# First six input blocks multiplied with x ahead of its norm: a fused two-block kernel on Trainium2

## Chip, cores and metric

One Trainium2 chip, one core. The metric is device microseconds (us) of one execution; lower is better. The engines are named as in the profile: PE (TensorE matmul), PEld (its weight loads), DVE (VectorE), ACT (ScalarE), POOL (GpSimd), SP (SyncE, which issues nearly all transfers).

## What is computed

Two transformer blocks on 512 tokens of width 1024, in float32. The part that the change touches is the start of the first block (the reference, cut):

```python
def rms_norm(x, g):
    y = xf * lax.rsqrt(jnp.mean(xf * xf, axis=-1, keepdims=True) + RMS_EPS)
    return (y * g).astype(x.dtype)

h = rms_norm(x, norm_mix)
p = h @ w_in                                   # 5,408 columns
p_rw = p_rw + (token_shift(p_rw) - p_rw) * mu_shift
r, k, v, wd, ad, gd, cb, cc, cx, ga, gb = jnp.split(p, offsets, axis=-1)
out_a = rwkv7_branch(r, k, v, wd, ad, gd, ...)   # a recurrence over tokens
out_b = short_conv_branch(cb, cc, cx, conv_w)
merged = sigmoid(ga + bg_a) * (out_a @ w_proj_a) + sigmoid(gb + bg_b) * (out_b @ w_proj_b)
x = x + merged @ w_out_mix
```

After this come cross-attention to a memory of 256 tokens, an MLP, and the second block (windowed attention and spatial gating). The norm's factor belongs to a token, so that (x * norm_mix) @ w_in can be multiplied by it afterwards, column by column of the transposed product.

## The kernel before

**Layout.** Activations lie transposed: 128 features on the partitions, 512 tokens along a row, eight such tiles for 1024 features. w_in is held as 43 blocks of 128 output columns. Each block is one `proj_in(blk)` (L228): eight contraction steps j of three matmuls 128x512 into one PSUM bank, 24 in all. The three are the terms of a float32 product in split form (`mm_fm`, L179): high part times high part (L182), weight-high times activation-low (L183), weight-low times activation-high (L184). `wload` (L168) fetches a block's weights in two halves of 256 KB (DMA L174 on SP's queue, five buffers `wraw`), and `split` (L150) makes of each half a high part by an ACT cast (L152, `whi`, four buffers) and a low part by a DVE subtraction (L153, `wlo`, three). With `early` POOL makes that subtraction (tiles `we`).

**Banks.** Three PSUM banks (`mm`) take these products, two (`sc`) sums, broadcasts and transposes, three (`ch`) the recurrence. A product may begin when the bank that it takes has been read out.

**Order.** A scheduler fixes each engine's instruction stream at build time, and an engine runs its stream strictly in that order. A wait at one instruction therefore holds all that stands behind it on that engine.

**The start.** x arrives in four transfers of 512 KB (`x0`, L120), then the first weights. ACT squares the eight x tiles (L203, L206), DVE and POOL add them into two accumulators (L207, L208), `sums` (L142) lets PE sum over the partitions, `rsqrt` (L130) takes eleven small DVE steps, `bcast` (L189) spreads the result over the partitions through PE, and eight DVE steps `hx` (L212) scale x, each split into `h`. Only then can a block of w_in begin, since every product reads `h`.

**The blocks.** Block 0 holds the two low-rank inputs, 1 and 2 the gate's; `prep(j)` (L283) for j = 0 to 3 takes three blocks for k, r and v, each followed by `shift` (L233: an ACT scaling `q`, then one DVE step L237 that mixes a token with the one before). `prep` also has head sums (L292), a low-rank product (`lora_mm`, L274), a broadcast (L314) and a chain of DVE and POOL steps that ends in `rkk` (L332). `prep_tail(j)` (L337) sums rkk (L340) and transposes v (`vs`, L344) on PE. After the fourth, 24 matmuls make the output gate gt (L369 to L371).

**The recurrence** runs in eight chunks of 64 tokens: `gram` (L386), an inverse that DVE iterates, and `chunk` (L431, matmuls L443 to L491), where each step waits for a DVE or ACT result. To keep PE busy the scheduler sets matmuls of independent blocks between those steps: gate b (blocks 15 to 22, tiles `bt`, L553), the convolution (23 to 34), w_proj_b and gate a (35 to 42, `tga`). After it come transposes of the memory (L586) and the product w_k.

Of the kernel before, what the change touches and what calls it, by code (L numbers as in the profile page):

```python
# [19 lines left out]
D = 1024  # L20
# [25 lines left out]
def fused_kernel(ctx, tc, a, out):  # L46
# [19 lines left out]
    def regionr(name):  # L66
        return reg.tile([128, 4, 2, T], F32R, tag="R", bufs=7, name=nm(name))
# [4 lines left out]
    def tt(name, shape=(128, T), dt=F32):  # L72
        return tp.tile(list(shape), dt, tag="t", bufs=10, name=nm(name))
# [4 lines left out]
    def mmbank():  # L78
        return ps.tile([128, T], F32, tag="mm", bufs=3, name=nm("mm"))
# [4 lines left out]
    def chbank():  # L84
        return ps.tile([128, T], F32, tag="ch", bufs=3, name=nm("ch"))
# [30 lines left out]

    vc = cst.tile([128, NVEC], F32, name="vc")
    x0 = reg.tile([128, DB, T], F32, tag="R", bufs=7, name="x0")
    for i in range(4):
        nc.sync.dma_start(x0[:, 2 * i:2 * i + 2], a["xT"][:, 2 * i:2 * i + 2])  # L120
        if i == 0:
            nc.sync.dma_start(vc, a["vecs"])

    def vcol(name, i=0, n=1):
        o = VOFF[name] + i
        return vc[:, o:o + n]
# [31 lines left out]
    def wsplit(raw, shape, early=False):  # L158
        if early:
            w = reg.tile([128, 2] + shape[1:], F32R, tag="G4", bufs=4, name=nm("we"))  # L160
            split(raw, w[:, 0], w[:, 1], eng=G)
            return w[:, 0], w[:, 1]
# [5 lines left out]
    def wload(tiles, k0, nk, early=False):  # L168
        ncol = tiles.shape[2]
        step = T // ncol  # L170
        parts = []
        for k in range(k0, k0 + nk, step):
            raw = wp.tile([128, step, ncol], F32, tag="wraw", bufs=5, name=nm("wraw"))
            nc.sync.dma_start(raw, tiles[:, k:k + step, :])  # L174
            hi, lo = wsplit(raw, [128, step, ncol], early)
            parts += [(hi[:, i, :], lo[:, i, :]) for i in range(step)]
        return parts

# [18 lines left out]
    hreg = [regionr("h0"), regionr("h1")]  # L197
    h = pairs(hreg, DB)
    accx = [tt("accx"), tt("accx")]
    for j in range(DB):  # L200
        acc = accx[j % 2]
        if j < 2:
            S.activation(acc, x0[:, j], AF.Square)  # L203
        else:
            sq = tt("sqx")
            S.activation(sq, x0[:, j], AF.Square)  # L206
            (V, G)[j % 2].tensor_tensor(acc, acc, sq, op=ALU.add)  # L207
    V.tensor_tensor(accx[0], accx[0], accx[1], op=ALU.add)  # L208
# [980 lines left out]
```

## Time and profile before

| | us |
|---|---|
| three runs | 1343.22, 1336.71, 1340.09 |
| median | 1340.09 |
| the profiled execution | 1343.95 |
| its span in the trace | 1342.1 |

The granted clock of PE over the span is 0.989 of full speed. PE is busy for 97% of the span, DVE for 61%, ACT for 39%, POOL for 13%. The chain of work that ended last is PE for 94%. How to read it: the page gives shares over the whole span, the waits say which engine stood still for what, the windows give busy time and granted clock of a stretch, and the timeline lists instructions by their start, where several of one form that follow each other are one row with their count.

### The profile page before, as it was taken

To read this page: it belongs to the slowest core of one execution; us is meant where nothing else is said; L and a number is where in the kernel's file an instruction comes from. 1 tells how busy PE (TensorE), PEld (TensorE's weight loads), DVE (VectorE), ACT (ScalarE), POOL (GpSimd) and SP (SyncE) were. 2 spreads that over 40 slices of the span, in tenths; PEclk is the share of its full clock that TensorE was granted. 3 is DMA by queue.
4 is the path that set the end of the run, shared out by engine and by line. 5 is a ranking of instruction groups with operands and counts; after the bars stand their busy time and mean duration, and the time that the engine had idled before them with its cause. 6 is when DMAs were issued, how large, how long until landed. Compare 5 with 4: busy or idle time off the path is not lost.

```text
span 1342.1 us, 18317 instructions
## 1 busy us (share of the span) xinstructions
PE 1302.3 (97%) x6626; PEld 1069.7 (80%) x6626; DVE 814.8 (61%) x1631; ACT 520.5 (39%) x940; POOL 174.4 (13%) x184
## 2 busy tenths in 40 slices
PE   3999999999999999999999999999999999999997
PEld 2777888888879888888888888888878777788886
DVE  5677484848466755566854645535676656663455
ACT  4444232322335443454532423323344465333342
POOL 5113002010120010002012020020232000100003
PEclk9999999989999999999999999999999999999999
DMA  4222331314314532143643634332234223233331
GB/s 143 87 79 67 101 104 43 110 44 123 90 63 150 173 110 94 64 149 94 186 152 110 194 112 145 128 96 87 94 126 142 79 63 125 87 97 101 94 118 63
DMA packets 85210, 143.95 MB, mean 107 GB/s; under 512 B 21472, under 2 KB 21600, under 8 KB 85120
## 3 DMA queue, kind: packets, MB, share of 16 engines
q1 hardware_dynamic: 85120, 142.78, 34.0%
q8 instruction: 52, 0.85, 0.3%
q14 instruction: 38, 0.31, 0.1%
HBM read 136.19 MB, written 5.24 MB: 105 GB/s over the span
## 4 chain that ended last, share of the span: by engine, by line
PE 94%; DVE 3%; POOL 1%; DMA 1%; issue 0%; ACT 0%; SPq 0%; DVEq 0%; ACTq 0%; POOLq 0%
PE mm L182 26%; PE mm L183 26%; PE mm L184 25%; PE mm L627 1%; PE mm L628 1%; PE mm L629 1%; PE sc L386 1%; PE ch L943 1%; PE ch L978 1%; PE ch L458 1%; PE ch L467 1%; DMA x<-in_xT 1%; PE sc L974 1%; PE ch L462 1%; PE ch L491 1%; PE ch L474 1%
## 5 line engine op out<-in xcount | busy, mean ns | idle before, releaser
L152 ACT CAST whi<-wraw 128x512 fp32r<-128x512 f32 x406 | 251.7, 621 | 551.7 <-PE mm L183 475.7
L153 DVE TENSOR_TENSOR wlo<-wraw,whi 128x512 fp32r<-128x512 f32 x406 | 298.4, 736 | 228.1 <-PE mm L184 118.6
L182 PE MATMUL mm<-h,whi 128*128 128x512 f32 x328 | 132.5, 404 | 1.0 <-DVE k L237 1.0
L183 PE MATMUL mm<-h,whi 128*128 128x512 f32 x328 | 131.4, 401 | 0.0
L184 PE MATMUL mm<-h,wlo 128*128 128x512 f32 x328 | 131.1, 400 | 0.0
L182 PE MATMUL mm<-x2g,whi 128*128 128x512 f32 x256 | 100.2, 391 | 0.0
L184 PE MATMUL mm<-x2g,wlo 128*128 128x512 f32 x256 | 99.7, 389 | 0.0
L183 PE MATMUL mm<-x2g,whi 128*128 128x512 f32 x256 | 99.6, 389 | 0.0
L182 PE MATMUL mm<-ff,whi 128*128 128x512 f32 x256 | 99.6, 389 | 0.0
L183 PE MATMUL mm<-ff,whi 128*128 128x512 f32 x256 | 99.6, 389 | 0.0
L184 PE MATMUL mm<-ff,wlo 128*128 128x512 f32 x256 | 99.6, 389 | 0.0
L182 PEld LDWEIGHTS mm<-h,whi 128*128 128x128 f32 x328 | 62.8, 192 | 16.2 <-DVE k L237 2.6
L183 PEld LDWEIGHTS mm<-h,whi 128*128 128x128 f32 x328 | 62.7, 191 | 13.1 <-issue 0.4
L184 PEld LDWEIGHTS mm<-h,wlo 128*128 128x128 f32 x328 | 62.5, 190 | 13.3 <-issue 0.5
L852 POOL TENSOR_TENSOR X<-X,d 128x512 f32<-128x512 f32 x24 | 39.3, 1637 | 220.8 <-DVE d L850 220.8
L658 POOL TENSOR_TENSOR gt<-gt,nsq 128x512 f32<-128x512 f32 x21 | 27.7, 1320 | 291.5 <-ACT nsq L657 284.0
L183 PE MATMUL mm<-h2a,whi 128*128 128x512 f32 x152 | 59.7, 393 | 0.4 <-DVE h2a L875 0.4
L184 PE MATMUL mm<-h2a,wlo 128*128 128x512 f32 x152 | 59.8, 393 | 0.0
L182 PE MATMUL mm<-h2a,whi 128*128 128x512 f32 x152 | 59.7, 395 | 0.0
L182 PE MATMUL mm<-h2b,whi 128*128 128x512 f32 x152 | 59.7, 392 | 0.0
L184 PE MATMUL mm<-h2b,wlo 128*128 128x512 f32 x152 | 59.5, 393 | 0.0
L183 PE MATMUL mm<-h2b,whi 128*128 128x512 f32 x152 | 59.5, 392 | 0.0
(465 smaller groups left out, 2700.7 us busy)
## 6 DMA issues: line engine op xcount, KB each, us to landing
wraw<-in_w_in SPq DMA_DIRECT2D x162, 256.0 KB, 2.6
wraw<-in_w_up SPq DMA_DIRECT2D x64, 256.0 KB, 2.6
wraw<-in_w_down SPq DMA_DIRECT2D x64, 256.0 KB, 2.8
adaraw<-in_w_ada SPq DMA_DIRECT2D x24, 512.0 KB, 3.7
wraw<-in_w_proj_b SPq DMA_DIRECT2D x16, 256.0 KB, 2.7
wraw<-in_w_k SPq DMA_DIRECT2D x16, 256.0 KB, 2.6
wraw<-in_w_proj_a SPq DMA_DIRECT2D x16, 256.0 KB, 2.7
wraw<-in_w_v SPq DMA_DIRECT2D x16, 256.0 KB, 2.7
```

The lines of the kernel that those rows point to most:

```text
L152: S.copy(hi, src)
L153: eng.tensor_tensor(lo, src, hi.bitcast(F32), op=ALU.subtract)
L182: PE.matmul(acc, lhsT=wh, rhs=xh, start=start and k == 0, stop=False)
L183: PE.matmul(acc, lhsT=wh, rhs=xl, start=False, stop=False)
L184: PE.matmul(acc, lhsT=wl, rhs=xh, start=False, stop=stop and k == n - 1)
L386: PE.matmul(pq[hd % 2][:, j * 128:(j + 1) * 128], lhsT=KB[p0:p0 + 64, j, n * 128:(n + 1) * 128], rhs=AR[p0:p0 + 64, j, n].rearrange("p q c ...
L458: PE.matmul(pu[ub:ub + 32, hs], lhsT=ZT[ub:ub + 32, c, hd, :], rhs=gsb[ub:ub + 32, hs], start=True, stop=True)
L462: PE.matmul(pg[ub + 32:ub + 64, hd * 64:(hd + 1) * 64], lhsT=gr[ub:ub + 32, hd, 32:64], rhs=VU[ub:ub + 32, tb, c, hd, :], start=False, sto ...
L467: PE.matmul(pu[ub + 32:ub + 64, hs], lhsT=ZT[ub + 32:ub + 64, c, hd, :], rhs=gsb[ub + 32:ub + 64, hs], start=True, stop=True)
L474: PE.matmul(pst[:, j * 128:(j + 1) * 128], lhsT=KBt[:, 2 * j:2 * j + 2, :].rearrange("p h f -> p (h f)"), rhs=VU[:, tb, c, 2 * j:2 * j + 2 ...
L658: G.tensor_tensor(self.acc, self.acc, sq, op=ALU.add)
L852: G.tensor_tensor(X[:, j], X[:, j], d, op=ALU.add)
```

## The change

Line numbers from here on are those of the changed file where a row of the order of instructions says so; elsewhere they are those of the kernel before.

- x arrives in six transfers (four of one tile, 256 KB, and two of 512 KB), with the first halves of the weights of blocks 0 to 5 between them and the second halves behind (`first_weights`, buffers `wraw`).
- `split` takes x itself with norm_mix as the scale (ACT makes the high part of x * norm_mix, DVE the low part: tiles `xg`), and the six blocks accumulate (`first_mm`) into six banks, the three `mm` and the three `ch`, one contraction step of all six after the other as x lands. The 12 weight halves are split into areas of their own (`wf`, and `we`).
- The squares are added up by DVE alone, one accumulator. Their `sums` stands on PE behind the fourth contraction step, the broadcast behind the fifth.
- The broadcast is copied to SBUF (`rxs`, ACT), DVE makes hx and h of all eight tiles, and after them six DVE multiplications (`pf`) that scale the six finished products out of their banks. `shift` of blocks 0 to 5 reads `pf` in SBUF in place of a bank.
- Gate b's blocks 15 and 16 stand ahead of block 0's shift, block 17 ahead of the fourth `prep_tail`, the other five where all eight stood.
- The `early` path with POOL's subtractions is gone.

No product is left out: PE's stream has 5466 rows in both (a row may be several matmuls of one form).

```diff
+NFIRST = 6
...
-    for i in range(4):
-        nc.sync.dma_start(x0[:, 2 * i:2 * i + 2], a["xT"][:, 2 * i:2 * i + 2])
+    nc.sync.dma_start(x0[:, 0], a["xT"][:, 0])
+    nc.sync.dma_start(vc, a["vecs"])
+    first_weights(0, 0)
+    first_weights(1, 0)
+    nc.sync.dma_start(x0[:, 1], a["xT"][:, 1])
+    for i, j in ((2, 2), (3, 3), (4, 4), (5, 6)):
+        first_weights(i, 0)
+        nc.sync.dma_start(x0[:, j:min(j + 2, DB) if j > 3 else j + 1],
+                          a["xT"][:, j:min(j + 2, DB) if j > 3 else j + 1])
+    for i in range(NFIRST):
+        first_weights(i, 1)
...
-    accx = [tt("accx"), tt("accx")]
+    first = [mmbank() for _ in range(3)] + [chbank() for _ in range(3)]
+    accx = tt("accx")
+    def first_split(half):
+        w4 = regionr("wf")
+        for blk in range(NFIRST):
+            if blk < 4:
+                w = w4[:, blk]
+            else:
+                w = reg.tile([128, 2, T], F32R, tag="G4", bufs=4, name=nm("we"))
+            split(raw0[blk, half].rearrange("p k c -> p (k c)"), w[:, 0], w[:, 1])
+            wf_[blk, half] = w
+    def first_mm(j):
+        for blk in range(NFIRST):
+            w = wf_[blk, j // 4]
+            cs_ = slice((j % 4) * 128, (j % 4 + 1) * 128)
+            mm_fm(first[blk], [(w[:, 0, cs_], w[:, 1, cs_])], [xg[j]], start=j == 0, stop=j == DB - 1)
     for j in range(DB):
-        acc = accx[j % 2]
...
+        split(x0[:, j], xg[j][0], xg[j][1], scale=vcol("norm_mix", j))
+        if j % 4 == 0:
+            first_split(j // 4)
...
-            (V, G)[j % 2].tensor_tensor(acc, acc, sq, op=ALU.add)
-    V.tensor_tensor(accx[0], accx[0], accx[1], op=ALU.add)
-    rxb = bcast(rsqrt(sums(accx[0]), TB, 1.0 / D, 1e-6))
+            V.tensor_tensor(accx, accx, sq, op=ALU.add)
+        if j < DB // 2:
+            first_mm(j)
+    ssx = sums(accx)
+    first_mm(DB // 2)
+    rxb = bcast(rsqrt(ssx, TB, 1.0 / D, 1e-6))
+    for j in range(DB // 2 + 1, DB):
+        first_mm(j)
+    rxs = tt("rxs")
+    S.copy(rxs, rxb)
     for j in range(DB):
         hf = tt("hx")
-        V.scalar_tensor_tensor(hf, x0[:, j], vcol("norm_mix", j), rxb, op0=ALU.mult, op1=ALU.mult)
+        V.scalar_tensor_tensor(hf, x0[:, j], vcol("norm_mix", j), rxs, op0=ALU.mult, op1=ALU.mult)
         split(hf, h[j][0], h[j][1])
+    pf = []
+    for blk in range(NFIRST):
+        f = tt("pf")
+        V.tensor_tensor(f, first[blk], rxs, op=ALU.mult)
+        pf.append(f)
...
+    def proj_in(blk):
+        if blk < NFIRST:
+            return pf[blk]
...
+    gate_b(0)
+    gate_b(1)
     sa = tt("sa")
-    shift(proj_in(0, True), 12, sa)
+    shift(proj_in(0), 12, sa)
...
         tail = prep(j, tail)
+    gate_b(2)
     prep_tail(3, *tail)
...
-    for j in range(DB):
-        S.activation(bt[:, j], proj_in(15 + j), AF.Tanh, bias=hbg[:, 8 + j:9 + j], scale=0.5)
+    for j in range(3, DB):
+        gate_b(j)
```

How the order of PE's instructions stands at three places. In its rows `mm_`, `sc_` and `ch_` are banks, and the numbers only tell one use of a name from another.

PE at the end of the first `prep`, kernel before (mm_541 is block 5, v of j = 0; L340 and L344 are prep_tail(0); L274 is the second low-rank product; mm_656 is r of j = 1):

```order
L184 MATMUL mm_541<-h_3_113,wlo_551 128x512
L340 MATMUL sc_582<-hsel,rkk_496 128x2 x4
L344 MATMUL sc_588<-ident,vs_498 128x128 x4
L274 MATMUL mm_618<-wa,lhl 128x512
L274 MATMUL mm_619<-wa,lhl 128x512
L182 MATMUL mm_656<-h_2_112,whi_659 128x512
```

The same place in the changed file (mm_638 is block 6, k of j = 1; L332 is the second low-rank product; L398 and L402 are prep_tail(0); mm_753 is r of j = 1):

```order
L195 MATMUL mm_638<-h_43_386,wlo_648 128x512
L332 MATMUL mm_715<-wa,lhl 128x512
L332 MATMUL mm_716<-wa,lhl 128x512
L398 MATMUL sc_679<-hsel,rkk_630 128x2 x4
L402 MATMUL sc_685<-ident,vs_632 128x128 x4
L193 MATMUL mm_753<-h_42_385,whi_756 128x512
```

Before, block 4 and block 5 (r and v of j = 0) stand between the chain's start and L340; now they are done long ahead, and of whole blocks only block 6 stands between the first low-rank product and L398.

PE at the end of the fourth `prep`, before (mm_1105 is v of j = 3, L369 to L371 the gate gt):

```order
L184 MATMUL mm_1105<-h_3_113,wlo_1115 128x512
L369 MATMUL mm_1172<-whi_1161,gsp_255 128x512
L340 MATMUL sc_1146<-hsel,rkk_1102 128x2 x4
L370 MATMUL mm_1172<-whi_1161,gsp_255 128x512
L371 MATMUL mm_1172<-wlo_1162,gsp_255 128x512
```

And in the changed file (mm_1243 is gate b's block 17, 24 matmuls of which the last two stand here; L428 to L430 are the gate gt):

```order
L194 MATMUL mm_1243<-h_43_386,whi_1252 128x512
L195 MATMUL mm_1243<-h_43_386,wlo_1253 128x512
L398 MATMUL sc_1281<-hsel,rkk_1199 128x2 x4
L402 MATMUL sc_1287<-ident,vs_1201 128x128 x4
L428 MATMUL mm_1307<-whi_1296,gsp_535 128x512
```

A whole block now stands between v of j = 3 and the sum over its rkk, where one matmul stood.

PE in the last chunk of the recurrence, before (L447 to L491 are the chunk's steps, mm_3655 is one of the last blocks of gate a):

```order
L458 MATMUL ch_2405<-gsb_2404,ZT_2129 32x64 x8
L182 MATMUL mm_3655<-h_2_112,whi_3658 128x512
L183 MATMUL mm_3655<-h_2_112,whi_3658 128x512
L184 MATMUL mm_3655<-h_2_112,wlo_3659 128x512
L182 MATMUL mm_3655<-h_2_112,whi_3658 128x512
L183 MATMUL mm_3655<-h_2_112,whi_3658 128x512
L462 MATMUL ch_2391<-VU,gram_2002 32x64 x8
```

And in the changed file (L517, L521, L526 and L550 are the chunk's steps L458, L462, L467 and L491; mm_3779 is the last block of gate a, L644 transposes of the memory, mm_3819 the first block of w_k):

```order
L517 MATMUL ch_2540<-gsb_2539,ZT_2264 32x64 x8
L644 MATMUL sc_3720<-ident,mt_2584 128x128 x4
L194 MATMUL mm_3779<-h_43_386,whi_3788 128x512
L644 MATMUL sc_3765<-ident,mt_2588 128x128 x4
L521 MATMUL ch_2526<-VU,gram_2137 32x64 x8
L195 MATMUL mm_3779<-h_43_386,wlo_3789 128x512
L526 MATMUL ch_2540<-gsb_2539,ZT_2264 32x64 x8
L193 MATMUL mm_3819<-memhl,whi_3822 128x256
L550 MATMUL ch_2506<-VU,gram_2137 64x64 x8
```

Of the independent blocks 83 matmuls still stood behind L491 of the last chunk, 16 amid its steps; now gate a's last block ends amid them, and w_k begins.

## Rows read from the trace of the kernel before

**Rows 1.** Page, busy time (share of the span) and instructions by engine.
```profile
PE 1302.3 (97%) x6626; PEld 1069.7 (80%) x6626; DVE 814.8 (61%) x1631; ACT 520.5 (39%) x940; POOL 174.4 (13%) x184
```
**Rows 2.** Waits of PE: instruction <- releaser: us in total, times, longest.
```profile
PE sc L146 <- DVE accx L208: 17.0, 1, 17.0
PE sc L192 <- DVE rq_y L139: 4.1, 2, 3.4
PE sc L340 <- DVE rkk L332: 2.3, 1, 2.3
...
PE ch L447 <- DVE state L481: 1.3, 1, 1.3
...
PE mm L182 <- DVE k L237: 1.0, 1, 1.0
```
**Rows 3.** Windows: busy time and count by engine, granted clock, transfer share, GB/s.
```profile
core 0: us, PE busy (x) PEld busy (x) DVE busy (x) ACT busy (x) POOL busy (x), PEclk, DMA share, GB/s
...
10.00:15.00 5.00, 0.00 (x0) 0.00 (x0) 2.88 (x3) 3.42 (x6) 4.90 (x5) 1.00 0.91 263
...
0.00:25.78 25.78, 3.91 (x16) 3.56 (x16) 10.33 (x26) 10.14 (x17) 13.44 (x32) 1.00 0.60 186
25.78:30.00 4.22, 4.22 (x10) 3.19 (x11) 4.22 (x7) 3.10 (x6) 1.79 (x3) 1.00 0.00 0
30.00:40.00 10.00, 10.00 (x45) 8.26 (x44) 7.10 (x13) 3.56 (x7) 2.06 (x3) 1.00 0.34 109
...
53.00:57.00 4.00, 4.00 (x15) 3.22 (x15) 1.84 (x11) 0.33 (x1) 0.00 (x0) 0.59 0.00 0
...
132.00:139.00 7.00, 6.89 (x23) 5.85 (x24) 1.62 (x3) 1.22 (x3) 1.91 (x4) 0.52 0.17 59
```
**Rows 4.** Timeline of the start: start, duration, instruction, count, idle before it.
```profile
4.88 1.15 ACT L203 ACTIVATE accx<-x 128x512 f32<-128x512 f32 x2 [2.80 <-DMA x<-in_xT]
9.38 0.69 DVE L207 TENSOR_TENSOR accx<-accx,sqx 128x512 f32<-128x512 f32 x1 [3.52 <-ACT sqx L206]
15.11 5.40 POOL L153 TENSOR_TENSOR we<-wraw,we 128x512 fp32r<-128x512 f32 x4
15.19 1.74 DVE L208 TENSOR_TENSOR accx<-accx,accx 128x512 f32<-128x512 f32 x1 [1.16 <-POOL accx L207]
24.33 2.06 DVE L212 SCALAR_TENSOR_TENSOR hx<-x,vc,sc 128x512 f32<-128x512 f32 x3 [2.23 <-PE sc L192]
26.31 1.89 DVE L153 TENSOR_TENSOR h<-hx,h 128x512 fp32r<-128x512 f32 x3
```
**Rows 5.** Timeline of the first `prep`, PE and DVE.
```profile
52.68 0.95 PE L292 MATMUL sc<-hsel,sq 128*128 128x2 f32 x8
57.10 0.69 DVE L153 TENSOR_TENSOR wlo<-wraw,whi 128x512 fp32r<-128x512 f32 x1 [1.25 <-PE mm L184]
66.56 0.74 DVE L237 SCALAR_TENSOR_TENSOR r<-mm,omu,q 128x512 f32<-128x512 f32 x1
67.82 1.69 DVE L332 SCALAR_TENSOR_TENSOR rkk<-r,vc,f 128x512 f32<-128x512 f32 x1
72.93 0.96 PE L274 MATMUL mm<-wa,lhl 64*128 64x512 f32 x6
```
**Rows 6.** Timeline of the end of the fourth `prep`.
```profile
129.37 0.39 PE L369 MATMUL mm<-whi,gsp 128*128 128x512 f32 x1
130.30 1.66 DVE L332 SCALAR_TENSOR_TENSOR rkk<-r,vc,f 128x512 f32<-128x512 f32 x1
132.10 1.74 PE L340 MATMUL sc<-hsel,rkk 128*128 128x2 f32 x8 [2.35 <-DVE rkk L332]
142.08 1.16 PE L386 MATMUL sc<-AR,KB 64*128 64x128 f32 x16
```
**Rows 7.** Timeline of PE in the last chunk.
```profile
382.33 0.76 PE L447 MATMUL ch<-state,AR 128*64 128x128 f32 x5 [1.26 <-DVE state L481]
391.36 1.15 PE L491 MATMUL ch<-VU,gram 128*64 128x64 f32 x16
```

More of the change, by code (lines that the diff above doesn't have):

```diff
@@ L118, in fused_kernel, with first_weights @@
     x0 = reg.tile([128, DB, T], F32, tag="R", bufs=7, name="x0")
-    for i in range(4):
-        nc.sync.dma_start(x0[:, 2 * i:2 * i + 2], a["xT"][:, 2 * i:2 * i + 2])
-        if i == 0:
-            nc.sync.dma_start(vc, a["vecs"])
+    raw0 = {}
+    def first_weights(blk, half):
+        w = wp.tile([128, 4, 128], F32, tag="wraw", bufs=5, name=nm("wraw"))
+        nc.sync.dma_start(w, a["w_in"][blk][:, 4 * half:4 * half + 4, :])
+        raw0[blk, half] = w
+    nc.sync.dma_start(x0[:, 0], a["xT"][:, 0])
[9 more added lines that the diff above has]
+        first_weights(i, 1)
     def vcol(name, i=0, n=1):
@@ L156, in split, with wsplit @@
             V.scalar_tensor_tensor(lo, src, scale, hi.bitcast(F32), op0=ALU.mult, op1=ALU.subtract)
[L158 to L162, printed above, removed]
+    def wsplit(raw, shape):
         hi = wp.tile(shape, F32R, tag="whi", bufs=4, name=nm("whi"))
@@ L166, in wsplit, with wload @@
         return hi, lo
-    def wload(tiles, k0, nk, early=False):
+    def wload(tiles, k0, nk):
         ncol = tiles.shape[2]
@@ L174, in wload @@
             nc.sync.dma_start(raw, tiles[:, k:k + step, :])
-            hi, lo = wsplit(raw, [128, step, ncol], early)
+            hi, lo = wsplit(raw, [128, step, ncol])
             parts += [(hi[:, i, :], lo[:, i, :]) for i in range(step)]
@@ L194, in bcast @@
         return p
-    hreg = [regionr("h0"), regionr("h1")]
-    h = pairs(hreg, DB)
-    accx = [tt("accx"), tt("accx")]
-    for j in range(DB):
-        acc = accx[j % 2]
-        if j < 2:
-            S.activation(acc, x0[:, j], AF.Square)
+    xgr = [regionr("xg0"), regionr("xg1")]
+    xg = pairs(xgr, DB)
+    first = [mmbank() for _ in range(3)] + [chbank() for _ in range(3)]
+    accx = tt("accx")
+    wf_ = {}
+    def first_split(half):
[12 more added lines that the diff above has]
+            mm_fm(first[blk], [(w[:, 0, cs_], w[:, 1, cs_])], [xg[j]], start=j == 0, stop=j == DB - 1)
+    for j in range(DB):
+        split(x0[:, j], xg[j][0], xg[j][1], scale=vcol("norm_mix", j))
+        if j % 4 == 0:
+            first_split(j // 4)
+        if j == 0:
+            S.activation(accx, x0[:, j], AF.Square)
         else:
@@ L206, in fused_kernel @@
             S.activation(sq, x0[:, j], AF.Square)
-            (V, G)[j % 2].tensor_tensor(acc, acc, sq, op=ALU.add)
-    V.tensor_tensor(accx[0], accx[0], accx[1], op=ALU.add)
-    rxb = bcast(rsqrt(sums(accx[0]), TB, 1.0 / D, 1e-6))
+            V.tensor_tensor(accx, accx, sq, op=ALU.add)
[8 more added lines that the diff above has]
+    S.copy(rxs, rxb)
+    hreg = [regionr("h0"), regionr("h1")]
+    h = pairs(hreg, DB)
     for j in range(DB):
         hf = tt("hx")
-        V.scalar_tensor_tensor(hf, x0[:, j], vcol("norm_mix", j), rxb, op0=ALU.mult, op1=ALU.mult)
+        V.scalar_tensor_tensor(hf, x0[:, j], vcol("norm_mix", j), rxs, op0=ALU.mult, op1=ALU.mult)
         split(hf, h[j][0], h[j][1])
+    pf = []
[3 more added lines that the diff above has]
+        pf.append(f)
     omu = cst.tile([128, 15], F32, name="omu")
@@ L226, in fused_kernel @@
     V.tensor_scalar(hbg, vcol("b_gate", 0, 16), 0.5, None, op0=ALU.mult)
-    def proj_in(blk, early=False):
+    def proj_in(blk):
+        if blk < NFIRST:
+            return pf[blk]
         p = mmbank()
-        mm_fm(p, wload(a["w_in"][blk], 0, DB, early), h)
+        mm_fm(p, wload(a["w_in"][blk], 0, DB), h)
         return p
@@ L237, in shift, with gate_b @@
         V.scalar_tensor_tensor(dst, p, omu[:, mi:mi + 1], q[:, 0:T], op0=ALU.mult, op1=ALU.add)
+    bt = reg.tile([128, DB, T], F32, tag="R", bufs=7, name="bt")
+    def gate_b(j):
+        S.activation(bt[:, j], proj_in(15 + j), AF.Tanh, bias=hbg[:, 8 + j:9 + j], scale=0.5)
+    gate_b(0)
+    gate_b(1)
     sa = tt("sa")
-    shift(proj_in(0, True), 12, sa)
+    shift(proj_in(0), 12, sa)
     S.activation(sa[0:64], sa[0:64], AF.Tanh)
@@ L254, in fused_kernel @@
         sg = tt("sg")
-        shift(proj_in(1 + i, i == 0), 13 + i, sg)
+        shift(proj_in(1 + i), 13 + i, sg)
         S.activation(sg, sg, AF.Tanh, scale=0.5)
@@ L551, in fused_kernel @@
         post(tb)
-    bt = reg.tile([128, DB, T], F32, tag="R", bufs=7, name="bt")
-    for j in range(DB):
-        S.activation(bt[:, j], proj_in(15 + j), AF.Tanh, bias=hbg[:, 8 + j:9 + j], scale=0.5)
+    for j in range(3, DB):
+        gate_b(j)
     ob = regionr("ob")
```

## The prediction

> **What bounds the kernel now.** I read the page's busy times first: PE works 97% of the span, DVE 61% [rows 1]. So the time is PE's work plus what PE loses by standing still or by its slower clock, and a change that keeps the number of matmuls, as this one does, can only win or lose in those two. The waits of PE come next [rows 2]. One wait towers: 17.0 us at the start for the sum of squares, then 3.4 us for the rsqrt chain. In the windows PE is busy 3.91 us of the first 25.78 [rows 3], so 21.9 us are lost before the first block. Two smaller waits lie further on, 1.0 us for k and 2.3 us for rkk at the end of the fourth `prep`, and 1.3 us in the recurrence.
>
> The clock shows in the pitch of the matmuls: 10 in 4.22 us just after the start, 0.42 us each, against 45 (and 44 weight loads) in 10.00 us later [rows 3], 0.222 to 0.227, which I take as 0.2255. These are the 1.2 and the 2.4 GHz level. After the 2.3 us wait the granted clock is 0.52 for the 7 us from 132 to 139 [rows 3]. An idle stretch therefore costs its own length and a slow stretch behind it.
>
> **The start.** x in tiles of 256 KB lets work begin early, but 3.5 MB (x and six half blocks) must land before the last of the first four steps' inputs is there. At 263 GB/s [rows 3] that takes 13 us after a first landing near 4 (4.88 with 512 KB pieces [rows 4]), so about 16.7. Meanwhile ACT has 29 casts and squares at 0.57 (two squares in 1.15 [rows 4]), 16.5 us, done near 23. DVE has 20 splits of x and weights and 7 additions, 27 at 0.63 (three in 1.89, one alone 0.69 [rows 4]), 17 us; with waits for data it has the last sum near 25. POOL leaves this stage, and with it the slow DVE steps beside POOL (1.74 in place of 0.69 [rows 4]).
>
> PE first gets scattered matmuls from about 6 us, is fed without gaps from 13.5 and, as before, spends some 4 to 5 us at the 0.42 pitch. I take the fourth step's end at 28. Then: column sums 0.95, fifth step 18 x 0.2255 = 4.1, broadcast 1.0, three steps 54 x 0.2255 = 12.2. The six blocks are done at 46.1. The rsqrt chain (3.4 us [rows 2]) lies beside the fifth step's 4.1, which covers it by 0.7. DVE makes h and `pf` (8 scalings, 8 subtractions, 6 multiplications, 22 x 0.66 = 14.5) from 34.6 to 49, beside the last three steps; the first bank is free near 45.5, when gate b's block 15 wants it. If that cover were gone it would cost 1 to 2 us.
>
> Gate b's two blocks follow, 48 x 0.2255 = 10.8, to 57.0. Then both low-rank products, head sums and broadcast (0.96 [rows 5], 0.96, 0.95, 1.05), block 6 (5.4), and a short wait for the bank that gate b's tanh empties (0.3): 66.6 at the end of the second low-rank product. Before, PE was there at 72.93 + 0.96 = 73.9 [rows 5], without gate b's 10.8 of work but with 1.5 of `prep_tail(0)` (head sums and transposes) that now lies behind. So PE is **ahead by 73.9 + 10.8 - 1.5 - 66.6 = 16.6 us**. The 21.9 us that were idle don't all come back, since data, casts and the slow clock still hold PE until about 18.
>
> **A new wait behind it.** L398 now needs rkk, and what ran beside that chain before, blocks 4 and 5 (10.8 us), is done already. From head sums to the end of rkk it took 69.51 - 52.68 = 16.8 us [rows 5], of which DVE stood 1.25 for PE. With the sums at 57.0, rkk is ready near 72.6. PE arrives at 66.6: **6.0 us idle**. Queued behind L398 are the v transposes and block 7; three `mm` banks are held by block 6 and the second low-rank product, so nothing else could run. I charge **2.8 us** for the slower clock behind it, a little under the 3.3 lost by 7 us at 0.52 [rows 3]. From here the order is that of before, period by period.
>
> One rule speaks against this step. r and v are now shifted out of SBUF instead of a bank, so that DVE reads two SBUF operands there. A step that reads two SBUF operands beside POOL is the last addition of squares, 1.74 us in place of 0.69 [rows 4], while `shift` from a bank takes 0.74 [rows 5]. I leave r at 0.74, since POOL's step of the same chain may be over by then; the other end is 1.0 more idle.
>
> The Trainium skill, page "SBUF — State Buffer", section "SBUF: two separate sides", says that a DVE step with two SBUF inputs and a GpSimd step that reads SBUF exclude each other for their whole length; the row of 1.74 agrees, and by it alone the sum below would be 1 us smaller.
>
> **The fourth `prep_tail`.** From 129.37 to 142.08 [rows 6] PE does 24 matmuls (5.4), head sums (0.95) and transposes (0.5), 6.8 us at full speed in 12.7. Block 17 now stands ahead of L398 and takes 5.4 us, while rkk ended 131.96 - 129.37 = 2.6 us after v [rows 6] and v's shift ends about 3 later. Wait and slow clock go: **5.9 us back**. At worst, v's shift is late and half returns.
>
> **The end of the recurrence.** The three gate blocks that fill now elsewhere are missing as filling. The steps from L447 to L491 took 9.0 us [rows 7] with 16 fill matmuls (3.6 us) between them; now only five stand there, and memory transposes. The chain of DVE and ACT copies does not shorten, so PE idles 1 to 3.6 us, can fall to the slow clock (up to 3.3 as above), and w_k's weight splits crowd DVE (0.7). Ends 1 and 9; I take **4.0**, nearer the low end because no single gap there exceeds the 1.3 of [rows 2].
>
> **Sum.** 16.6 - 6.0 - 2.8 + 5.9 - 4.0 = **9.7 us gained**. The profiled execution of 1343.95 becomes 1334; it stands 3.9 above the median of the three runs, so the median becomes 1330.
>
> **Rivals.**
> 1. *The gain is given back in part.* The wait for rkk is 2 us longer (the SBUF step, the slow clock's full 3.3) and the last chunk costs 7 to 9. Gain 3 to 5: 1335 to 1337. For it: both terms are estimates, and filling only moves work. Against: no wait over 1.3 us in the recurrence now.
> 2. *Slower: PE stays at 1.2 GHz through the first stage.* It is fed piecemeal by transfers, ACT and DVE, and each gap can bring the slow level back. From 18.5 on some 114 matmuls are left; each at 0.42 costs 0.195 more, up to 22 us, so 12 slower than before: 1352. It decides where 50 stay slow, since 50 x 0.195 is the whole gain. For it: 0.52 after a wait of only 2.3 us. Against: before, PE left the slow level 4 us after its first block, with DVE and ACT feeding it as closely.
> 3. *More is won.* The wait for rkk brings no slow stretch (+2.8), a bank wait less, and the last chunk loses 1 (+3): 16 gained, 1323. For it: after the 1.0 us wait for k the granted clock was 0.59 for only the 4 us from 53 [rows 3]. Against: 6.0 is over twice the 2.35 that brought 7 slow us.
> 4. *The early products don't hide the start*, because the accumulators keep the banks until h and `pf` are done: PE would wait some 4 us more at gate b, gain 6: 1334. DVE's order shows `pf` of the first bank right behind the seventh and eighth hx, against it.
>
> The second rival's mechanism stands on the page "TensorE: Matmul & The Clock Gate" of the Trainium skill, section "HAM oscillation": a kernel that computes in bursts with transfer waits between them is put back to the low level in each. The trace of before shows it once, behind one wait, and no row shows it in a stage fed like this one.
>
> **How the numbers follow.** Runs differ by about 0.5% (6.7 us), so a gain under that can't be told from none. Forecast, gain 7 to 14 us, 0.52; rival 3, 0.12; rivals 1 and 4 and smaller losses within the bound, 0.24; rival 2 in full 0.08 and other losses of over 6.7 us 0.04. Faster 0.64, same 0.24, slower 0.12. The range leaves out the 0.12 of loss and some 0.08 at the far end of gain: 1319 to 1343.
>
> **What would show it.** Right: first matmuls near 6 us, PE idle in the first 26 us down to about 10; a wait of L398 for rkk near 66 to 73, of about 6 us; no wait for rkk after the fourth `prep`, `gram` about 10 us earlier in work than before; some 1 to 3 us of new waits at L517 to L550. Wrong: the column sums later than 32 us or the granted clock at 0.5 between 20 and 46 (rival 2); a wait of PE for `pf` (rival 4); no wait at L398 (rival 3); waits of over 5 us in the last chunk (rival 1). The forecast as a whole is wrong if the median lies over 1337 or under 1320.

## The result and the profile after

The changed kernel takes 1330.64 us (median of 6 runs, 1326.92 to 1334.01) against 1340.14 (6 runs, 1336.71 to 1343.22): ratio 0.9926, 95% interval 0.9903 to 0.9948, so the gain is clear of the noise. Measured once more beside another 11 runs of the kernel before it is 1330.84 against 1342.16, ratio 0.9922 (0.9893 to 0.9952). The forecast was 1330 in a range of 1319 to 1343.

First the page, busy times of the changed kernel (span 1328.0 us, execution 1330.0):

```profile
span 1328.0 us, 18328 instructions
...
PE 1300.2 (98%) x6626; PEld 1066.0 (80%) x6626; DVE 824.2 (62%) x1652; ACT 525.7 (40%) x949; POOL 165.3 (12%) x177
```

PE's idle time is span less busy time: 1328.0 - 1300.2 = 27.8 us, where it was 1342.1 - 1302.3 = 39.8 [rows 1]. So 12.0 of the 14.1 us between the two spans are idle time that is gone. Which, the waits of PE say (changed kernel):

```profile
PE mm L193 <- ACT wf L167: 5.9, 1, 5.9
PE sc L398 <- DVE rkk L390: 5.3, 1, 5.3
PE ch L506 <- DVE state L540: 1.3, 1, 1.3
PE mm L193 <- ACT ob L167: 1.2, 1, 1.2
...
PE sc L203 <- DVE rq_y L154: 0.7, 1, 0.7
```

The 17.0 us and most of the rsqrt chain's wait [rows 2] have become one wait of 5.9 for the first cast. The wait for rkk is there twice as long, but it is another one: L398 waits once, at the first `prep_tail`, and no longer at the fourth. The timeline of PE, with DVE and POOL around rkk, gives the places:

```profile
5.95 0.80 PE L193 MATMUL mm<-xg,wf 128*128 128x512 f32 x1 [5.95 <-ACT wf L167]
...
10.25 0.64 PE L195 MATMUL mm<-xg,wf 128*128 128x512 f32 x1
...
11.36 0.39 PE L194 MATMUL ch<-xg,wf 128*128 128x512 f32 x1
...
25.78 0.95 PE L161 MATMUL sc<-ones,accx 128*128 128x1 f32 x8
...
30.82 1.05 PE L203 MATMUL sc<-ident,rq_y 128*128 128x128 f32 x8
...
43.98 0.39 PE L193 MATMUL mm<-h,whi 128*128 128x512 f32 x1
...
63.95 0.97 PE L332 MATMUL mm<-wa,lhl 64*128 64x512 f32 x6
...
67.18 0.74 DVE L287 SCALAR_TENSOR_TENSOR r<-pf,omu,q 128x512 f32<-128x512 f32 x1
...
68.00 1.56 POOL L388 TENSOR_TENSOR AR<-r,pp 128x512 f32<-128x512 f32 x1 [1.96 <-DVE r L287]
...
68.44 1.66 DVE L390 SCALAR_TENSOR_TENSOR rkk<-r,vc,f 128x512 f32<-128x512 f32 x1
...
70.25 1.84 PE L398 MATMUL sc<-hsel,rkk 128*128 128x2 f32 x8 [5.33 <-DVE rkk L390]
...
73.01 0.79 PE L193 MATMUL mm<-h,whi 128*128 128x512 f32 x1
...
136.32 0.48 PE L428 MATMUL mm<-whi,gsp 128*128 128x512 f32 x1
...
141.99 1.16 PE L445 MATMUL sc<-AR,KB 64*128 64x128 f32 x16
```

The duration of one matmul shows the clock: 0.63 us until 10.9 and 0.39 from 11.4 on, so PE left the 1.2 GHz level 5.4 us after its first matmul, although it was fed in pieces. The granted clock in the windows (columns as in [rows 3]) doesn't show this: it reads 1.00 from the start, also where a matmul takes 0.63 us, as it did before at 0.42 us a matmul (25.78 to 30.00 in [rows 3]). At the start the durations decide. What the windows show is PE busy for 19.73 of the first 25.78 us, the slow stretch behind the wait for rkk, and the one that is gone at 132 to 139:

```profile
0.00:25.78 25.78, 19.73 (x72) 14.22 (x73) 19.98 (x38) 19.52 (x33) 3.54 (x24) 1.00 0.81 271
...
10.00:15.00 5.00, 5.00 (x19) 3.30 (x18) 5.00 (x9) 5.00 (x10) 0.00 (x0) 1.00 1.03 403
...
70.00:75.00 5.00, 4.75 (x17) 4.03 (x18) 1.59 (x4) 1.88 (x3) 0.11 (x1) 0.50 0.11 43
...
132.00:139.00 7.00, 7.00 (x39) 5.96 (x38) 3.30 (x6) 3.59 (x6) 2.48 (x5) 1.00 0.44 143
```

The forecast's steps, each as PE's lead over the kernel before at the same work (a block of w_in ahead counts 24 x 0.2255 = 5.4 us):

| at | worked out | measured |
|---|---|---|
| end of the second low-rank product (64.9) | 16.6 | 73.9 + 10.8 - 1.5 - 64.9 = 18.3 |
| last matmul of the last low-rank product (116.0; before 115.7) | 16.6 - 6.0 - 2.8 = 7.8 | 115.7 + 10.8 - 116.0 = 10.5 |
| `gram` begins (141.99; before 142.08) | 13.7 | 142.08 + 16.2 - 141.99 = 16.3 |
| first transpose of gt behind the recurrence (394.36; before 410.62) | 9.7 | 16.3 |
| end of the span | 9.7 | 14.1 |

For the last chunk, the timeline of PE in the changed kernel:

```profile
382.17 0.76 PE L506 MATMUL ch<-state,AR 128*64 128x128 f32 x5 [1.26 <-DVE state L540]
...
390.43 1.15 PE L550 MATMUL ch<-VU,gram 128*64 128x64 f32 x16 [0.28 <-DVE VU L528]
...
394.36 0.60 PE L666 MATMUL sc<-ident,gt 128*128 128x128 f32 x4
```

From L506 to L550 it is 8.26 us, where it was 9.03 [rows 7], and the new idle time is 0.28: the last chunk lost nothing. In the seven other runs below that leave five gate blocks to the recurrence it takes 8.25 to 8.27 us, each with the same 0.28 of idle time. What is lost between 394 and the end, 2.2 us, is nothing that the change touches: in the change measured again that part takes 931.9 us, before 931.5. A slow stretch (granted clock 0.76 from 1040 to 1047 us, 1.00 at the same place before) is part of it.

**Runs and the granted clock.** The runs of one kernel differ by 10 us, and they do so along the mean granted clock of each run:

| granted clock | before, us (runs) | the change, us |
|---|---|---|
| 0.994 | 1336.4 to 1338.3 (15) | 1324.0 |
| 0.992 | 1338.5 to 1341.4 (8) | 1326.9 |
| 0.990 | 1342.2 to 1343.1 (8) | 1330.0, 1330.3 |
| 0.988 | 1344.6 to 1345.8 (8) | 1334.0, 1333.5 |

At an equal clock the change is 11 to 14 us shorter, about the 12.0 of idle time. The medians of the first comparison differ by 9.5, since the change's six runs stood at 0.987 to 0.993, while the times of those before are, by this table, those of 0.989 to 0.994. The profiled execution before stood at 0.989, among the lower ones. Such a comparison has a limit: an edit that brings or removes a slow stretch moves the mean clock itself, and at an equal clock that part of its worth doesn't show.

### The profile page after: what moved, and what is told of

Same layout as the page of the kernel before. It is cut to its first block, busy times and chain, and to the rows that moved or that the text cites. A ratio compares the mean times of both kernels' runs of the same rounds, so it can differ in the third digit from the quotient of the medians.

```text
span 1328.0 us, 18328 instructions
## 1 busy us (share of the span) xinstructions
PE 1300.2 (98%) x6626; PEld 1066.0 (80%) x6626; DVE 824.2 (62%) x1652; ACT 525.7 (40%) x949; POOL 165.3 (12%) x177
## 4 chain that ended last, share of the span: by engine, by line
PE 93%; DVE 4%; issue 1%; POOL 0%; DMA 0%; ACT 0%; SPq 0%; DVEq 0%; ACTq 0%; POOLq 0%
PE mm L193 25%; PE mm L194 25%; PE mm L195 25%; PE mm L687 1%; PE mm L685 1%; PE mm L686 1%; PE sc L445 1%; DVE wlo L168 1%; PE ch L1001 1%; PE ch L1036 1%; PE ch L517 1%; PE ch L526 1%; PE sc L1032 1%; PE ch L550 1%; PE ch L521 1%
## 5 line engine op out<-in xcount | busy, mean ns | idle before, releaser
L167 ACT CAST whi<-wraw 128x512 fp32r<-128x512 f32 x398 | 246.6, 622 | 530.4 <-PE mm L194 460.1
L168 DVE TENSOR_TENSOR wlo<-wraw,whi 128x512 fp32r<-128x512 f32 x398 | 290.1, 731 | 217.4 <-PE mm L195 113.3
L193 PE MATMUL mm<-h,whi 128*128 128x512 f32 x296 | 118.7, 401 | 0.0
L194 PE MATMUL mm<-h,whi 128*128 128x512 f32 x296 | 117.5, 397 | 0.0
L195 PE MATMUL mm<-h,wlo 128*128 128x512 f32 x296 | 117.1, 396 | 0.0
L193 PEld LDWEIGHTS mm<-h,whi 128*128 128x128 f32 x296 | 56.2, 190 | 13.7 <-DVE k L287 1.1
L195 PEld LDWEIGHTS mm<-h,wlo 128*128 128x128 f32 x296 | 56.2, 190 | 12.0 <-issue 0.2
L194 PEld LDWEIGHTS mm<-h,whi 128*128 128x128 f32 x296 | 56.2, 190 | 11.2 <-issue 0.2
```

The costliest lines, as they stand in the source:

```text
L193: PE.matmul(acc, lhsT=wh, rhs=xh, start=start and k == 0, stop=False)
L194: PE.matmul(acc, lhsT=wh, rhs=xl, start=False, stop=False)
L195: PE.matmul(acc, lhsT=wl, rhs=xh, start=False, stop=stop and k == n - 1)
```

## The experiments

### Block 17 back behind the recurrence

```diff
-    gate_b(2)
     prep_tail(3, *tail)
...
-    for j in range(3, DB):
+    for j in range(2, DB):
```

> Block 17 of gate b goes back to its old place behind the recurrence; everything else is the change. Theory (the block covers the wait for rkk at the end of the fourth prep): PE waits about 2.4 us for rkk there again and runs at 1.2 GHz for some 7 us behind it, so the run is 5.9 us longer than the change, about 1336 to 1337. Rival (block 17 only moved work, and the recurrence's end pays for the missing filling): no longer than the change, 1327 to 1331, with a shorter last chunk.

Median 1332.15 (5 runs), ratio to the kernel before 0.9929 (0.9905 to 0.9952). The waits of PE, with line 398 as before:

```profile
PE sc L398 <- DVE rkk L390: 7.7, 2, 5.3
```

The second wait, 2.4 us, is back at 134.6, with a slow stretch of 3.4 us behind it. Against the change the profiled idle time is 1332.4 - 1303.1 = 29.3, 1.5 more: the wait for `ob` in the recurrence (1.2) has gone. At 0.988 to 0.992 the runs lie 0 to 2 us above the change's, and the medians differ by 1.5. So the theory's wait is right, and its time is missed by about 4 us. Of its price of 5.9 the trace shows 4.1: from the last low-rank product (118.2) to `gram` (142.93) PE gains 1.7 us on the kernel before, where the change gains 5.8. The rival's shorter last chunk didn't come either (9.92 us). Why the medians show less than the trace is open: that the returned block is worth something as filling is not shown, since the recurrence without it takes as long as the change's (the table under the last run).

### A fourth gate block in the wait

```diff
     def prep(j, tail):
+        if j == 1:
+            gate_b(2)
         k = tt("k")
...
-    gate_b(2)
+    gate_b(3)
     prep_tail(3, *tail)
...
-    for j in range(3, DB):
+    for j in range(4, DB):
```

> One more block of gate b stands ahead of block 6, between the first low-rank product and the first prep_tail; the fourth prep_tail keeps a gate block of its own, and the recurrence is left with four. Theory (PE's 5.3 us wait for rkk is lack of independent work, and the slow clock from 70 to 76 us follows from it): the wait and the slow stretch go, 5.3 + 2.9 = 8 us less than the change, about 1322. Rival A (DVE makes the new block's weight splits ahead of rkk, so the chain gets later by as much as it covers): a wait of 2 us or more stays, gain 3 or less. Rival B (the recurrence's end is out of filling): waits of 3 to 6 us in the last chunk and a gain of 2 to 5.

Median 1332.94 (6 runs), ratio 0.9941 (0.9918 to 0.9964): no gain over the change. The wait went, from 5.3 to 0.8 us; the waits of PE in this run (L400, L523 and L646 are L398, L521 and L644 of the change):

```profile
PE ch L523 <- DVE VU L521: 1.0, 1, 1.0
PE sc L646 <- DVE mt L602: 0.9, 1, 0.9
...
PE sc L400 <- DVE rkk L392: 0.8, 1, 0.8
```

The slow stretch did not go with it. Behind the 0.8 us for rkk (and 0.2 for vs) PE runs at 1.2 GHz from 72 to 82 us, longer than in the change:

```profile
75.00:80.00 5.00, 5.00 (x18) 4.23 (x17) 1.83 (x11) 0.00 (x0) 0.00 (x0) 0.50 0.00 0
```

Idle time is 1335.0 - 1309.6 = 25.4, 2.4 less than the change's, but busy time is 9.4 more for the same 6626 matmuls. That is the clock. The windows show where else: three stretches of the recurrence, first of the change, then of this run.

```profile
200.00:240.00 40.00, 39.87 (x322) 33.01 (x321) 20.75 (x48) 10.46 (x18) 6.44 (x10) 0.96 0.22 55
270.00:310.00 40.00, 39.88 (x320) 33.31 (x319) 16.78 (x29) 7.97 (x15) 6.35 (x9) 0.91 0.22 58
370.00:410.00 40.00, 38.46 (x366) 34.92 (x365) 32.80 (x77) 18.28 (x35) 7.08 (x5) 1.00 0.30 96
```

```profile
200.00:240.00 40.00, 39.74 (x265) 32.66 (x263) 15.82 (x38) 9.17 (x16) 6.44 (x10) 0.79 0.20 53
270.00:310.00 40.00, 39.37 (x322) 32.55 (x321) 24.17 (x57) 8.93 (x15) 7.38 (x10) 1.00 0.23 63
370.00:410.00 40.00, 36.14 (x295) 31.99 (x295) 29.28 (x68) 14.30 (x27) 6.27 (x5) 0.79 0.19 61
```

PE falls to 0.79 in two of them, in 200 to 240 while busy for 39.74 of 40 us. The cost that the forecast charged to the change's last chunk, waits and a slow clock for lack of filling, came here, with one block less. Rival B has the right place and waits of the right size (4.2 us in the recurrence, 3.0 in the change); it had no word of the clock, and its gain of 2 to 5 did not come.

### Column sums behind all six blocks

```diff
-    ssx = sums(accx)
-    first_mm(DB // 2)
-    rxb = bcast(rsqrt(ssx, TB, 1.0 / D, 1e-6))
-    for j in range(DB // 2 + 1, DB):
+    for j in range(DB // 2, DB):
         first_mm(j)
+    rxb = bcast(rsqrt(sums(accx), TB, 1.0 / D, 1e-6))
```

> Column sums, rsqrt and broadcast stand behind all six blocks on PE instead of amid them. Theory (the queueing hides not just the rsqrt chain but all of DVE's making of h and pf, 15 us, beside the last four steps): h and pf come some 16 us later, PE waits for h at gate b's blocks, and the run is 13 to 17 us longer than the change, about 1344 to 1348, no faster than before. Rival (only the rsqrt chain and the broadcast are hidden by it): 3.4 + 1.0 us and a short slow stretch, 1335 to 1337.

Median 1342.86 (10 runs), ratio 1.0026 (1.001 to 1.0042): 12 us over the change, and the gain is gone. Its waits and its timeline of PE:

```profile
PE mm L193 <- ACT h L167: 10.4, 1, 10.4
```

```profile
42.18 0.95 PE L161 MATMUL sc<-ones,accx 128*128 128x1 f32 x8
45.45 1.33 PE L203 MATMUL sc<-ident,rq_y 128*128 128x128 f32 x8 [2.32 <-DVE rq_y L154]
```

The column sums end at 43 us and the broadcast at 47, and PE then stands 10.4 us for h, until 57.18, where the change goes on at 43.98. So what the queueing hides is DVE's and ACT's making of h, not just the rsqrt chain (2.3). The theory's mechanism holds; the 12 us lie just under its 13 to 17.

### Blocks 15 and 16 back behind the recurrence

```diff
-    gate_b(0)
-    gate_b(1)
     sa = tt("sa")
...
-    for j in range(3, DB):
+    for j in (0, 1, 3, 4, 5, 6, 7):
```

> Blocks 15 and 16 of gate b go back behind the recurrence, block 17 stays where the change has it; the six early blocks stay. Theory (the early products only free PE; what fills it until DVE has scaled and shifted them is the two gate blocks): PE stands idle from about 44 us until the first low-rank product near 50, and again for rkk until about 70, so that block 7 begins near 72 to 73 as in the change but without the 10.8 us of gate work: 1341, no faster than before. Rival (the early products are the gain, wherever the gate blocks stand): 1331 to 1333.

Median 1337.35 (10 runs, 1336.6 to 1351.67, at granted clocks from 0.988 down to 0.975), ratio 1.000 (0.9974 to 1.0026). Waits of PE (L330 and L396 are L332 and L398 of the change):

```profile
PE sc L396 <- DVE rkk L388: 6.2, 1, 6.2
PE mm L330 <- ACT lhl L167: 5.2, 1, 5.2
```

PE stands from 44 to 49.6 for the low-rank input and from 63 to 69.2 for rkk, and its granted clock is at the 1.2 GHz level from 63 to 80. Six runs lie at 1336.6 to 1337.5, four at 1345.6 to 1351.7 with a lower clock, on either side of the theory's 1341; the rival's 1331 to 1333 falls, since the change's slowest run took 1335.3. By the ratio the six early products alone give nothing that can be told from the kernel before: the time that they free is a gain only because two independent blocks stand ready for it.

### The gate's DVE work later

```diff
-        f = tt("pf")
+        f = ft("pf") if blk in (1, 2) else tt("pf")
...
     gate_b(0)
-    gate_b(1)
     sa = tt("sa")
...
+        if j == 0:
+            gate_b(1)
         r = tt("r")
         shift(proj_in(4 + 3 * j), j, r)
...
     for j in range(4):
         tail = prep(j, tail)
+        if j == 1:
+            ...
```

The last lines are the loop that shifts and splits blocks 1 and 2, moved from its place ahead of `prep`.

> The DVE work that rkk of j = 0 does not need is taken out of its way: shift and split of blocks 1 and 2 come behind the second prep, and gate b's block 16 behind the first low-rank product, so that k's head sums stand on PE some 5 us earlier. Theory (the 5.3 us wait is set by DVE's chain from the broadcast to rkk): rkk ends 3 to 4 us earlier, the wait falls to 1 to 3 us, and the run is 2 to 5 us shorter than the change. Rival A (POOL's and ACT's steps set the chain): rkk stays near 70, no gain. Rival B (the wait shrinks but the slow clock behind it stays or grows, as with the fourth gate block): the wait falls and the time does not, within 1 us of the change.

Median 1329.65 (6 runs), ratio 0.9912 (0.9884 to 0.9939). Waits of PE (L391 is L398):

```profile
PE sc L391 <- DVE rkk L383: 2.0, 1, 2.0
PE mm L193 <- DVE k L287: 1.3, 1, 1.3
```

L398's counterpart begins at 66.07 instead of 70.25. That agrees with a chain set by DVE; but k's head sums on PE come earlier too, and the run doesn't tell the two apart. The shorter wait wins next to nothing, for the slow stretch behind it is longer, 66 to 80 us against 70 to 76 in the change, and a new wait of 1.3 for k brings another at 97 to 104:

```profile
66.00:80.00 14.00, 13.93 (x46) 11.15 (x47) 6.29 (x19) 3.19 (x5) 0.11 (x1) 0.51 0.12 43
```

So `gram` begins at 146.11, 4.1 us later than in the change's profile with the same work done. At equal clocks the runs are 1 to 3 us shorter than the change's (1327.5 and 1328.5 at 0.990), the medians differ by 1.2 or less, and the intervals overlap: no gain over the change is shown. Rival B came nearest.

### Block 17 in the first wait, and both waits filled

On top of the run before:

```diff
     def prep(j, tail):
+        if j == 1:
+            gate_b(2)
         k = tt("k")
...
-    gate_b(2)
     prep_tail(3, *tail)
```

> The order of the run with the gate's DVE work later, and block 17 of gate b moved from the fourth prep_tail to a place ahead of block 6; the recurrence keeps five gate blocks as in the change. Theory (the 1.2 GHz stretch from 69 us on follows from PE standing idle there): no wait for rkk at the first prep_tail and no slow stretch between 60 and 85 us; the 2.4 us wait at the fourth comes back with a slow stretch of 3 to 7 us behind it. PE idle in all 24 to 25 us against the change's 27.8, time 1325 to 1328. Rival (the head sums and transposes of prep_tail bring the slow level by themselves): a slow stretch of 7 us or more near 70 although PE never waits there, and 1329 to 1332.

Median 1331.88 (6 runs), ratio 0.9922 (0.9898 to 0.9947). The window from 60 to 85 us, first of the change, then of this run, with two further on:

```profile
60.00:85.00 25.00, 19.67 (x91) 15.77 (x90) 16.78 (x32) 11.04 (x19) 6.74 (x11) 0.86 0.14 41
```

```profile
60.00:85.00 25.00, 24.99 (x125) 20.20 (x124) 18.93 (x35) 11.61 (x19) 7.04 (x10) 1.00 0.20 64
90.00:105.00 15.00, 13.16 (x61) 10.71 (x61) 8.68 (x23) 7.18 (x13) 0.11 (x1) 0.77 0.19 65
132.00:140.00 8.00, 5.65 (x25) 4.43 (x24) 4.19 (x6) 2.06 (x4) 3.99 (x7) 0.79 0.27 85
```

PE doesn't stand there and keeps 2.4 GHz through the head sums and transposes, so the change's slow stretch at 70 follows from its idle time. But the wait of 2.4 us at the fourth `prep_tail` and one of 1.8 us for k near 93 each bring a slow stretch of their own, idle time is 26.6 us where the theory had 24 to 25, and nothing is won: its time of 1325 to 1328 is missed, and the rival's came true without its mechanism.

With a gate block ahead of the fourth `prep_tail` again, and four left to the recurrence:

> As the run before, with a gate block ahead of the fourth prep_tail too, so that the recurrence keeps four. Theory (with fewer filling blocks PE runs the small matmuls of the recurrence with less between them, and the granted clock falls there more often): no wait at either prep_tail, but slow stretches of 25 us or more between 200 and 410 us as in the run with a fourth gate block, mean granted clock 0.985 to 0.987, time 1328 to 1332. Rival (those stretches came of chance or of the 1 us wait at 70): granted clock 0.990 or more, 1321 to 1325.

Median 1335.73 (11 runs), ratio 0.9945 (0.9926 to 0.9963), granted clocks of 0.981 to 0.988. Windows of this run:

```profile
270.00:310.00 40.00, 39.87 (x292) 33.23 (x291) 16.68 (x36) 7.07 (x12) 7.40 (x10) 0.79 0.18 48
370.00:410.00 40.00, 35.37 (x298) 31.00 (x296) 27.84 (x61) 13.79 (x26) 6.29 (x5) 0.79 0.18 56
```

Neither `prep_tail` waits for rkk, and the recurrence pays, at 0.79 in two stretches and with 4.6 us of idle time in the last: the second run to do so with four gate blocks left. The theory's mechanism held, and the time came out 4 us worse than it said.

### x in 512 KB pieces

```diff
-    nc.sync.dma_start(x0[:, 0], a["xT"][:, 0])
+    nc.sync.dma_start(x0[:, 0:2], a["xT"][:, 0:2])
     nc.sync.dma_start(vc, a["vecs"])
...
+    for i in range(3):
+        first_weights(2 * i, 0)
+        first_weights(2 * i + 1, 0)
+        nc.sync.dma_start(x0[:, 2 * i + 2:2 * i + 4], a["xT"][:, 2 * i + 2:2 * i + 4])
```

> x arrives in four transfers of 512 KB, as before the change, with the six half weights still between them. Theory (from 10 us on ACT and DVE, busy without gaps, set the pace, not the transfers): the first matmul comes 0.5 to 1.5 us later, the six blocks end within 1 us of the change's 44.0. Rival (x in small pieces is what lets PE begin early): the six blocks end 2 us or more later.

One run, 1324.25 us at a granted clock of 0.994, where the change has 1324.0. The first matmul comes at 7.17 instead of 5.95, gate b's first at 44.47 instead of 43.98. Timed:

> x in four transfers of 512 KB, as in the single look, now timed. Theory (the 1324 of the single look is the change at a granted clock of 0.994, where the change has 1324.0 too): median within 2 us of the change's, 1329 to 1332, and at equal granted clock the same time within 1 us. Rival (x in larger pieces is faster): median 1324 to 1326.

Median 1329.48 (6 runs), ratio 0.9906 (0.9883 to 0.993), five of them at 0.990 with 1329.2 to 1330.1, where the change has 1330.0 and 1330.3. The size of x's pieces makes no difference that can be told, as both theories said. From 10 to 20 us ACT, DVE and PE are all busy without a gap in the change, so the transfers are not what is waited for there; which of the three sets the pace isn't shown.

### Additions of squares shared with POOL

```diff
-            V.tensor_tensor(accx, accx, sq, op=ALU.add)
+            (V, G)[j % 2].tensor_tensor(accx, accx, sq, op=ALU.add)
```

> Every other addition of squares goes back to POOL. Theory (DVE is held up beside a POOL step that reads SBUF, as in the kernel before, where an addition took 1.2 to 1.7 us instead of 0.7): DVE's splits beside it take 1.2 to 1.8 us, the column sums come later than in the change, the six blocks end at 44.5 to 47. Rival (four additions less on DVE): column sums and the end of the six blocks 1 to 2.5 us earlier.

One run, 1330.72 us. The column sums begin at 27.88 instead of 25.78, gate b at 46.08 instead of 43.98. DVE's groups from 5 to 27 us say why, the change's first (busy time, mean ns of one):

```profile
L171 DVE SCALAR_TENSOR_TENSOR xg<-x,vc,xg 128x512 fp32r<-128x512 f32 x8 | 6.0, 747 | 0.4 <-ACT xg L170 0.3
```

```profile
L171 DVE SCALAR_TENSOR_TENSOR xg<-x,vc,xg 128x512 fp32r<-128x512 f32 x8 | 8.5, 1076 | 0.9 <-ACT xg L170 0.9
```

Beside four POOL additions of 1.29 to 1.61 us DVE's splits of x take 44% longer on average, and four additions less do not make up for it. The Trainium skill, page "SBUF — State Buffer", section "SBUF: two separate sides", has DVE steps with two SBUF inputs and GpSimd steps that read SBUF exclude each other; 1076 against 747 ns agrees. In these two traces, taking POOL out of the stage is worth 2.1 us there.

### The change again

> The change itself once more, unaltered. Theory (the 1.2 GHz stretches behind a wait are fixed by the kernel, those in the recurrence fall differently from run to run): the wait for rkk is 5.3 us again with a slow stretch of 3 to 14 us behind it, the other slow stretches lie elsewhere or have other lengths, and the profiled executions differ by as much as the stretches do; median 1328 to 1333. Rival (slow stretches are part of the kernel's order): the same places and lengths within 1 us.

1330.84 (6 runs). The wait for rkk is 5.3 us again, and the slow stretch behind it as long as before, 70 to 77. Those in the recurrence are not the same; windows of this run:

```profile
200.00:240.00 40.00, 39.87 (x322) 33.13 (x321) 20.67 (x49) 11.07 (x19) 6.44 (x10) 0.96 0.22 57
270.00:310.00 40.00, 39.87 (x293) 33.18 (x293) 14.88 (x26) 7.07 (x12) 6.34 (x9) 0.79 0.18 47
```

The same order of instructions ran at 0.91 from 270 to 310 in the first profile and at 0.79 in this one, with PE busy for 39.9 of 40 us in both. That is up to 40 x (0.91 - 0.79) = 4.8 us of PE's time; the two spans differ by 3.5.

Put together, the profiled executions of all runs show what the recurrence costs with fewer blocks to fill it: the time from the first `gram` to the first transpose of gt, with gate blocks over five taken off and a missing one added, at 5.4 us each.

| gate blocks left | profiles | us | granted clock |
|---|---|---|---|
| 8 | kernel before | 252.3 | 0.97 |
| 7 | blocks 15 and 16 back | 248.0 | 0.99 |
| 6 | block 17 back | 252.7 | 0.97 |
| 5 | the change twice, six other runs | 247.7 to 257.1, mean 252.6 | 0.96 to 1.00 |
| 4 | fourth gate block, both waits filled | 263.5, 265.9 | 0.93 |

Five blocks cost nothing against eight; a fourth taken out of the recurrence costs 6 us or more. With five the stretch still differs by 9.4 us between executions, nearly as much as the whole gain: 247.7 and 250.8 are one kernel (x in 512 KB pieces), 252.4 and 257.0 another (the change).

## Why the prediction came out right, step by step

- **The start** was sized at 16.6 us and gave 18.3. The six blocks ended at 43.98 instead of 46.1. Transfers moved 403 GB/s from 10 to 15 us, where the estimate took 263, and the column sums came at 25.8 instead of 28. PE idles for 6.0 of the first 25.78 us, not 10. That the rsqrt chain and the making of h hide beside the last steps is shown by the sums-last run: without it 12 us.
- **The new wait** was forecast at 6.0 us near 66 to 72 and is 5.3 from 64.9 to 70.25. That DVE's chain sets it agrees with the run with the gate's DVE work later. Its slow stretch, 2.8 forecast, is there from 69 to 76 and cost 2.5: the lead falls by 7.8 from 18.3 to 10.5, and 5.3 of that is the wait. The run with block 17 in the wait shows that it follows from the idle time. That a shorter wait would bring a shorter stretch is not so: 10 us at the low level behind 0.8 us, 14 behind 2.0, 6 behind 5.3.
- **The SBUF operand of shift**: r takes 0.74 us, as taken. POOL's step stood beside rkk (1.66), not beside r.
- **The fourth `prep_tail`**: 5.9 forecast; the lead grows from 10.5 to 16.3, 5.8. The run that undoes it loses 4.1 of that in its trace and 1.5 us between the medians; the slow stretch that came back with the wait was 3.4 us long, not 7.
- **The end of the recurrence, 4.0 us, is the step that failed.** The reasoning was that DVE's and ACT's copies set the last chunk's steps, so that missing filling turns into idle time. The steps got shorter instead, 8.26 us for 9.03: PE's filling itself had paced them, and the memory transposes that moved in sufficed. Of the 1 to 3 us of new waits came 0.28. Over the whole recurrence eight profiles with five blocks average 252.6 us, as much as before (252.3). The loss came only with one more block taken, in both runs with four gate blocks left. What stood unused behind the last chunk before agrees: 83 matmuls, by the timeline 59 of gate a and 24 of w_k's first block; three blocks take 72 of them, four would take 96.
- **From the profile to the median** 3.9 us were taken off, since the profiled execution stood that far above the median. The change's profiled execution stood 0.6 below its own. The two profiles are 14.0 us apart, the medians 9.5: the failed step and this hid each other. That the median met 1330 to 0.6 us is luck.
- **Rivals.** PE did not stay at 1.2 GHz in the first stage: 0.39 us a matmul from 11.4 us on. No wait of PE for `pf` appears. A part given back in the last chunk is what four gate blocks would have given, not five. Of the rival that more is won, the last chunk's part came true and the missing slow stretch did not. The second rival counts one slow stretch behind a wait in the trace of before; there are two (0.52 from 132, 0.59 from 53 [rows 3]).

Not tried: filling from work that the recurrence doesn't use, as w_k's product, which would need the memory's norm earlier. No version beat the change by more than its measurement can tell; the gate's DVE work later (1329.65) and x in 512 KB pieces (1329.48) come nearest, both within the spread of the change's runs.

## What to carry to other kernels

A norm's factor that belongs to the token can be applied behind the product, so that matmuls begin as the input lands; but what that frees is worth only as much as there is independent work to put there while the scaled input is made, and the reduction has to be queued amid the early products to hide that making. Filling is a stock: a block spent on one wait is missing at another, and where the stock runs out the price here was waits and a lower granted clock. Shortening a wait without closing it gained nothing that could be told here, since the slow stretch behind it did not get shorter. Compare runs at equal granted clock, beside the medians, before a difference of a few us is put down to an edit; what the edit itself does to the clock shows in the medians and windows alone.

## What the runs showed of the hardware

The granted clock falls to the 1.2 GHz level for parts of the recurrence while PE is busy for 39.7 to 39.9 of 40 us, with small matmuls (32x64 to 128x128) between the 128x512 ones, which are 72 of 320 from 270 to 310 us in the change. That stretch stood at 0.91 in one execution of the change and at 0.79 in another; over the whole recurrence the mean was 0.96 to 1.00 with five gate blocks left and 0.93 with four. The section "HAM oscillation" of the page "TensorE: Matmul & The Clock Gate" of the Trainium skill tells of the fall behind waits for transfers; here it also comes in a stretch with no more than 0.3 us of idle time. Behind a wait the length of the slow stretch doesn't follow the length of the wait (0.8 us: 10 us; 2.0: 14; 2.4: 3.4; 5.3: 6). Which run falls when is not fixed: one kernel gives 1336.4 us at a mean granted clock of 0.994 and 1345.8 at 0.988.
